# A two-number tile moved from the constants' pool to the temporaries' pool, so that the split weights start at multiples of 64 bytes

## The chip, the core and the metric

The kernel runs on one core of a Trainium2 chip. The metric is the device time of one execution in microseconds (us), the median of several runs. TensorE (PE) multiplies matrices, VectorE (DVE) and ScalarE (ACT) work element by element, SyncE (SP) issues most transfers from the main memory (HBM). Tiles lie in SBUF, 128 partitions wide; an address below is a byte address within each partition, the same on all 128.

## The reference

A decoder trunk of two layers on 256 tokens of 1024 numbers, all in float32. Every sublayer is wrapped in a norm, a modulation by a condition `c`, and a gated residual.

```python
def gated_post_add(x, y, g_post, gate, weight):
    return x + weight * gate[:, None, :] * rms_norm(y, g_post)

for layer in range(DEPTH):                       # DEPTH = 2
    ...
    y = swiglu_ffn(h, ffn_w_in[layer, 0], ffn_w_out[layer, 0])   # 1024 -> 2 x 2816 -> 1024
    x = gated_post_add(x, y, g[0, 1], mod[:, 0, 2], 0.5)
    ...
    if layer < n_a:
        y = short_conv_mixer(h, a_w_in[layer], a_conv[layer], a_w_out[layer])
    else:
        y = nsa_mixer(h, kv_cmp, kv_slc, kv_win, b_w_in[layer - n_a], b_w_out[layer - n_a])
    ...
    y = swiglu_ffn(h, ffn_w_in[layer, 1], ffn_w_out[layer, 1])
    ...
```

So there are four feed-forward sublayers, a short convolution, a sparse attention with its key and value side, and the modulations `silu(c) @ ada_w`.

## The kernel before

The tokens lie along the free dimension (256 columns) and the features on the 128 partitions. Each float32 product is made of three matmuls in the type fp32r: a weight block is split into a high part `whi` and the rest `wlo`, the activations into `hh`/`hl` (or `Hh`/`Hl` for the inner 2816 features), and `mm3` (L213) adds `hh` times `whi` (L215), `hl` times `whi` (L216) and `hh` times `wlo` (L217) in PSUM. In these the weights are the stationary operand (128 rows, 128 columns, loaded by a weight load of its own) and the activations are the moving operand (256 columns). Every matmul thus comes with a new weight load. Only where the values of the attention are projected (L652 to L654) the two are exchanged: `hh` and `hl` are loaded as weights and `whi` and `wlo` move.

The weights come in blocks of 2048 columns, loaded into `raw` (three buffers, SP's queue, L82). ScalarE copies a unit of 1024 columns into `whi` (L94), VectorE subtracts it from `raw` into `wlo` (L106); there are six buffers of each. VectorE also makes the modulations' products from blocks `graw` (L169). The norms sum squares by matmuls in which the data is the stationary operand and a single column of `ones` moves (`colsum`, L276); the attention's transposes (L878 to L880 and others) use an identity matrix that is part of the tile `sm`.

Four pools are stacked in SBUF in this order: `const` (x, z, hh, hl, then small tiles), `wp` (raw, whi, wlo), `tmp`, `gp` (graw), and behind these one that is exchanged (`hp` with Hh and Hl, `ap` for the attention). Each tile takes a multiple of 32 bytes. The tile `sxt` (two numbers for each partition, the sums of x squared; 8 bytes, so 32 with the rounding) is made in `const` (L986), written twice outside and inside of `sum_x_fin` (L1023, L287) and read by VectorE where the next norm's sums are worked out (`nc.vector.tensor_add(w, a1, self.sx)`, L381).

The order of the work is written out by hand; the pools set addresses and waits, not the order.

Of the kernel before, what the change touches and what calls it, by code (L numbers as in the profile page):

```python
# [9 lines left out]
F32 = mybir.dt.float32  # L10
# [12 lines left out]

# scale, shift and gate of each sublayer (and of the keys' and values' side) among the modulations
ADA = [(1, 0, 2), (4, 3, 5), (7, 6, 8), (10, 9, None), (19, 18, 11), (13, 12, 14), (16, 15, 17)]


class Trunk:
# [22 lines left out]

# [1 line left out]
    def w_init(self):  # L53
# [32 lines left out]
    def w_hi(self, upto):  # L86
        """the high parts, a unit ahead of the low ones"""
        while self.n_hi < min(upto, len(self.units)):
            i, u = self.units[self.n_hi]
            self.w_dma(i + 1)  # L90
            if i not in self.raw:
                return
            hi = self.wp.tile([128, 1024], F32R, name="whi", bufs=self.UNITS)
            self.nc.scalar.activation(hi, self.raw[i][:, u * 1024:u * 1024 + 1024], AF.Copy)  # L94
            self.his[self.n_hi] = hi
            self.n_hi += 1
# [18 lines left out]
    def w_whole(self):  # L115
        """the next block that is used as it is, and the function that frees it"""
        i = self.whole[0]
        self.w_dma(i + 1)

        def free():  # L120
            self.whole.pop(0)
            self.raw.pop(i)
            self.w_dma(i + 1 + self.RAW)
        return self.raw[i], free
# [7 lines left out]
    def w_ahead(self, more=0):  # L132
        """splits into what the units before the last taken one leave"""
        self.w_split(self.n_use + self.UNITS - 1 + more)

# [1 line left out]
    def g_init(self):  # L137
        """blocks of two columns of the modulations; scale and shift of a sublayer go together"""
        o = []
        for sub in range(7):  # L140
            sc, sh, gt = ADA[sub]
            o += [((sc, k), (sh, k)) for k in range(KC)]
            if gt is not None:
                o += [((gt, k), (gt, k + 1)) for k in range(0, KC, 2)]
        self.g_order = o
        self.g_raw = {}
        self.n_gd = self.n_g = 0
        self.credit = 0.0
        self.g_hold = False
        self.g_count = dict.fromkeys(range(20), 0)  # L150
        self.g_done = set()
# [28 lines left out]
    def g_fin(self, m, k0, k1):  # L180
        """with the bias; scales and gates times the norms' weights"""
        nc = self.nc
        v = self.mod[:, m, k0:k1]
        nc.vector.tensor_add(v, v, self.modb[:, m, k0:k1])
        if m >= 18:
            if m == 19:
                nc.vector.scalar_tensor_tensor(v, v, 1.0, self.kvg[:, k0:k1], op0=OP.add, op1=OP.mult)
        else:
            l, r = divmod(m, 9)
            s, p = divmod(r, 3)  # L190
            if p == 1:
                nc.vector.scalar_tensor_tensor(v, v, 1.0, self.ng[:, l, s, 0, k0:k1], op0=OP.add, op1=OP.mult)
            elif p == 2:
                nc.vector.scalar_tensor_tensor(v, v, 1.0 if s == 1 else 0.5, self.ng[:, l, s, 1, k0:k1],
                                               op0=OP.mult, op1=OP.mult)
        self.g_done.add(m)
# [14 lines left out]

# [1 line left out]
    def mm3(self, out, wh, wl, xh, xl, start, stop):  # L213
# [5 lines left out]
    def proj(self, hh, hl, n=1, nc_=2, each=None, out=None):  # L219
        """n weight blocks of [8 k, nc_ * 128 columns]; k is the outer loop. One bank for each."""  # L220
        out = out or [self.ps.tile([128, 2, S], F32, name="gu", bufs=4) for _ in range(n)]
# [24 lines left out]

# [1 line left out]
    def tiny(self, name):  # L248
        return self.tmp.tile([128, 2], F32, name=name)

    def inverse(self, s, name, late=False):
        """(s / D + eps) ** -0.5 of sums s [128, 2]: the mean of root / v and 1 / root, in which the root's error cancels"""
        nc = self.nc
# [12 lines left out]
    def spread(self, r, tag):  # L266
        """[128, 2] of the tokens -> [128, 256], the same on every partition"""
        o = self.ps.tile([128, S], F32, name=tag, bufs=4 if tag == "gu" else 2)
        for h in range(2):
            self.nc.tensor.transpose(o[:, h * 128:h * 128 + 128], r[:, h:h + 1].to_broadcast([128, 128]), self.ident)  # L270
        return o

    def colsum(self, o, v, start, stop):
        """o [128, 2] += the sums of v [128, 256] over the partitions, token 128 h + p at [p, h]"""
        for h in range(2):
# [3 lines left out]
    def sum_x(self):  # L279
        """sum of x ** 2 per token"""  # L280
        nc = self.nc
# [29 lines left out]
    def post_chunk(self, d, y):  # L311
        """z = y * gate * g and the sums of y ** 2, z ** 2 and x z"""
        nc = self.nc
# [12 lines left out]
    def post_mid(self):  # L326
        """the sums over all but the last chunk"""
        yy = self.ps.tile([128, 2], F32, name="st", bufs=2)
# [8 lines left out]
    def post_steps(self, nxt, keep=False):  # L337
        """x += r z; nxt: None or (scale, shift, hh, hl, blocks of the first wave) of the next sublayer.
        Without a first wave the steps are for the caller to spread over other work."""
        nc = self.nc  # L340
# [34 lines left out]
        ma, mb, hh, hl = nxt[:4]  # L375
        # the sum of (x + r z) ** 2 is x2 + 2 r xz + r ** 2 z2
        a1, w, a2, a3 = (self.tiny(n) for n in ("a1", "wx", "a2", "a3"))
# [49 lines left out]

# [1 line left out]
    def ffn(self, ia, fresh_x, nxt, kv=False):  # L429
        """ia: index of the sublayer's shift among the modulations"""  # L430
        nc = self.nc
# [157 lines left out]

# [1 line left out]
    def swap(self, name):  # L591
        """the large part of the memory to a new pool"""
        self.big.close()
        return self.big.enter_context(self.tc.tile_pool(name=name, bufs=1))
# [19 lines left out]
    def kv_proj(self):  # L614
# [4 lines left out]
        def each():  # L619
            """after each half of a block: a step of the queries' side"""  # L620
            half[0] ^= 1
            self.w_ahead(-1 - half[0])
            next(self.steps, None)
# [3 lines left out]
        for e in range(2):  # L627
            b = self.proj(hh, hl, each=each)[0]
            # group g on both halves of the partitions, the upper half one token ahead
            kc = self.BD[:, 4 * e:4 * e + 4].rearrange("p (a b) n -> p a (b n)", a=2)  # L630
# [30 lines left out]
    def blocks_of(self, e):  # L661
        """the compressed blocks' inputs [128 (2 tokens, 64), 16 token pairs, 4 groups, 15 blocks]"""
        at = 1024 * e
# [7 lines left out]
    def compress(self):  # L671
        """hidden units of the compressed blocks, (group, block) on partitions"""
        nc = self.nc
# [33 lines left out]
    def cmp_keys(self):  # L707
        """compressed keys [128 (2 groups, 64), 2 pairs, 32 (2 groups, 16 blocks)], block diagonal"""
        nc = self.nc
# [39 lines left out]
    def cmp_soft(self, a):  # L749
        """compressed branch: gated probabilities, transposed: [128 (4 chunks, 2 heads, 16 blocks), 2, 256 queries]"""  # L750
        nc = self.nc
# [31 lines left out]
    def q_half(self, i, u):  # L783
        """queries over -8, two heads (of groups 2 a and 2 a + 1) for each chunk; half of the products of two chunks"""
        nc = self.nc
# [190 lines left out]
    def run(self):  # L976
# [8 lines left out]
        self.sc = self.gp.tile([128, D], F32, name="sc")  # L985
        self.sx = c.tile([128, 2], F32, name="sxt")  # L986
        self.mod = c.tile([128, 20, 8], F32, name="mod")
# [97 lines left out]
def lay(inp):  # L1085
    """The inputs as the kernel wants them laid out; no arithmetic."""
    f = {n: np.asarray(v) for n, v in inp.items()}
# [17 lines left out]
    def cols128(w):  # L1105
        """[1024, 1024] -> blocks [128 p, 2 column chunks, 8 k, 128]"""
        v = w.reshape(KC, 128, 4, 2, 128)
        return ca(v.transpose(2, 1, 3, 0, 4)).reshape(4, 128, 2048)

    def cols256(w, pairs):  # L1110
        """[1024, n] -> blocks [128 p, 8 k, 256] of the columns that pairs names"""
        v = w.reshape(KC, 128, -1).transpose(1, 0, 2)
# [30 lines left out]
def consts(heads):  # L1143
    """Constants of the shapes alone: distances, penalties and masks."""
    big = 1e32
# [32 lines left out]
```

## Time and profile before

| | |
|---|---|
| runs | 1080.97, 1084.96, 1086.55 us; median 1084.96 us |
| profiled execution, from first to last instruction | 1084.8 us (the profile gives no other time of it) |
[...]
| TensorE busy | 96% of the span, 8438 matmuls |
| VectorE, ScalarE busy | 79%, 51% |
| HBM | 241 GB/s over the span |

"Busy" counts an instruction from its start to its end. Matmuls overlap each other: one of them takes 0.28 us from start to end, but the next one starts long before that. How fast TensorE gets on is seen only from how many matmuls start in a stretch of time.

### The profile page before, as it was taken

How to read it: one execution, taken by the hardware profiler on the slowest of the kernel's cores; microseconds unless marked ns; L12 is line 12 of the kernel's file. 1: busy time of each engine (PE TensorE's matmuls, PEld its weight loads, DVE VectorE, ACT ScalarE, POOL GpSimd, SP SyncE). 2: the span in 40 equal slices, each digit the busy share in tenths (PEclk: the TensorE clock that was granted, in tenths of full speed). 3: DMA queues.
4: the chain of work that ended last, by engine and by line, in shares of the span. 5: the costliest groups of instructions: out<-in, count | busy, mean ns of one | idle time of the engine just before them, and what ended most of it. 6: DMA issues, size and time to landing. Idle time of an engine off the chain costs nothing.

```text
span 1084.8 us, 20601 instructions
## 1 busy us (share of the span) xinstructions
PE 1042.1 (96%) x8438; PEld 1014.2 (93%) x8438; DVE 857.3 (79%) x1618; ACT 550.9 (51%) x1006; POOL 5.0 (0%) x12
## 2 busy tenths in 40 slices
PE   4999999999999999999999999999999999999996
PEld 4899999999989999998999999998887789999996
DVE  6879889799888988897898878968678698555553
ACT  3544454444556444554644444633578746444541
POOL 0000000000000000000000000010000000000000
PEclk9999999989989999999999999999999989999998
DMA  9899989727644988896298885766532134555531
GB/s 379 348 350 376 347 322 366 295 79 272 232 157 176 369 342 316 298 349 246 96 385 335 332 312 214 280 225 237 229 113 83 55 135 165 197 190 193 195 118 39
DMA packets 38063, 264.30 MB, mean 244 GB/s; under 512 B 4304, under 2 KB 5584, under 8 KB 6736
## 3 DMA queue, kind: packets, MB, share of 16 engines
q1 hardware_dynamic: 37584, 261.94, 64.2%
q8 instruction: 66, 1.08, 0.4%
q0 software_dynamic: 384, 1.05, 0.4%
q14 instruction: 29, 0.24, 0.1%
HBM read 260.87 MB, written 1.05 MB: 241 GB/s over the span
## 4 chain that ended last, share of the span: by engine, by line
PE 89%; DVE 7%; ACT 2%; issue 1%; DMA 1%; DVEq 0%; SPq 0%; ACTq 0%
PE gu L215 18%; PE gu L217 17%; PE gu L216 17%; PE y L215 9%; PE y L216 9%; PE y L217 9%; DVE graw L169 2%; PE st L276 2%; PE y L684 1%; PE gu L235 1%; PE gu L825 1%; DVE wlo L106 1%; DVE e L298 1%; PE y L891 1%; DMA x<-in_x_dram 1%
## 5 line engine op out<-in xcount | busy, mean ns | idle before, releaser
L215 PE MATMUL gu<-hh,whi 128*128 128x256 f32 x1592 | 447.9, 281 | 0.0
L216 PE MATMUL gu<-hl,whi 128*128 128x256 f32 x1592 | 446.2, 280 | 0.0
L217 PE MATMUL gu<-hh,wlo 128*128 128x256 f32 x1592 | 446.1, 280 | 0.0
L106 DVE TENSOR_TENSOR wlo<-raw,whi 128x1024 fp32r<-128x1024 f32 x319 | 379.1, 1221 | 60.4 <-ACT whi L94 60.4
L94 ACT ACTIVATE whi<-raw 128x1024 fp32r<-128x1024 f32 x319 | 323.6, 1054 | 47.7 <-PE y L216 31.0
L215 PEld LDWEIGHTS gu<-hh,whi 128*128 128x128 f32 x1592 | 301.4, 189 | 0.0
L216 PEld LDWEIGHTS gu<-hl,whi 128*128 128x128 f32 x1592 | 301.3, 189 | 0.0
L217 PEld LDWEIGHTS gu<-hh,wlo 128*128 128x128 f32 x1592 | 300.9, 189 | 0.0
L215 PE MATMUL y<-Hh,whi 128*128 128x256 f32 x768 | 217.1, 283 | 3.0 <-ACT st L318 3.0
L216 PE MATMUL y<-Hl,whi 128*128 128x256 f32 x768 | 216.5, 282 | 0.0
L217 PE MATMUL y<-Hh,wlo 128*128 128x256 f32 x768 | 216.4, 282 | 0.0
L169 DVE SCALAR_TENSOR_TENSOR graw<-graw,sc 128x1024 f32<-128x1024 f32 x160 | 194.1, 1218 | 0.0
L215 PEld LDWEIGHTS y<-Hh,whi 128*128 128x128 f32 x768 | 145.4, 189 | 3.4 <-ACT st L318 3.4
L216 PEld LDWEIGHTS y<-Hl,whi 128*128 128x128 f32 x768 | 145.5, 189 | 0.0
L217 PEld LDWEIGHTS y<-Hh,wlo 128*128 128x128 f32 x768 | 145.5, 189 | 0.0
L445 ACT ACTIVATE e<-gu 128x256 f32<-128x256 f32 x88 | 33.4, 380 | 197.0 <-PE gu L217 197.0
L446 DVE TENSOR_TENSOR e<-gu,e 128x256 f32<-128x256 f32 x88 | 37.2, 423 | 56.9 <-ACT e L445 56.7
L316 ACT ACTIVATE st<-y 128x256 f32<-128x256 f32 x42 | 16.1, 383 | 76.9 <-PE y L217 76.9
L302 ACT ACTIVATE hh<-e,mod 128x256 fp32r<-128x256 f32 x36 | 18.3, 510 | 61.8 <-DVE e L298 61.8
L319 DVE TENSOR_TENSOR st<-z,x 128x256 f32<-128x256 f32 x42 | 17.8, 424 | 36.0 <-ACT z L317 35.8
L450 ACT ACTIVATE Hh<-e 128x256 fp32r<-128x256 f32 x88 | 36.1, 410 | 17.6 <-DVE e L446 17.5
L451 DVE TENSOR_TENSOR Hl<-e,Hh 128x256 fp32r<-128x256 f32 x88 | 37.0, 420 | 7.8 <-ACT Hh L450 7.8
(197 smaller groups left out, 992.4 us busy)
## 6 DMA issues: line engine op xcount, KB each, us to landing
raw<-in_wi_dram SPq DMA_DIRECT2D x85, 1024.0 KB, 6.1
graw<-in_ada_dram SPq DMA_DIRECT2D x80, 1024.0 KB, 7.3
raw<-in_wo_dram SPq DMA_DIRECT2D x44, 1024.0 KB, 5.4
raw<-in_cu_dram SPq DMA_DIRECT2D x8, 1024.0 KB, 6.0
raw<-in_kvw_dram SPq DMA_DIRECT2D x6, 1024.0 KB, 7.3
raw<-in_bb_dram SPq DMA_DIRECT2D x4, 1024.0 KB, 5.2
raw<-in_ao_dram SPq DMA_DIRECT2D x4, 1024.0 KB, 4.8
raw<-in_w_dram SPq DMA_DIRECT2D x4, 1024.0 KB, 4.8
```

Source lines behind the costliest of these rows:

```text
L94: self.nc.scalar.activation(hi, self.raw[i][:, u * 1024:u * 1024 + 1024], AF.Copy)
L106: self.nc.vector.tensor_sub(lo, self.raw[i][:, u * 1024:u * 1024 + 1024], hi.bitcast(F32))
L169: nc.vector.scalar_tensor_tensor(w, w, 1.0, self.sc, op0=OP.mult, op1=OP.mult, accum_out=self.mod[:, m, k:k + 1])
L215: mm(out, wh, xh, start=start, stop=False, skip_group_check=True)
L216: mm(out, wh, xl, start=False, stop=False, skip_group_check=True)
L217: mm(out, wl, xh, start=False, stop=stop, skip_group_check=True)
L276: self.nc.tensor.matmul(o[:, h:h + 1], v[:, h * 128:h * 128 + 128], self.ones[:, 0:1], start=start and h == 0, stop=stop and h == 1, skip_ ...
L302: self.nc.scalar.activation(hh[:, k, :], t, AF.Identity, bias=self.mod[:, mb, k:k + 1])
L445: nc.scalar.activation(sg, b[:, 0, :], AF.Silu)
L446: nc.vector.tensor_mul(hf[f], b[:, 1, :], sg)
L450: nc.scalar.activation(H[:, f, :], t, AF.Copy)
L451: nc.vector.tensor_sub(L[:, f, :], t, H[:, f, :].bitcast(F32))
```

## The change

The tile `sxt` is made in the pool `tmp`, with one buffer, where it was made in `const`. The rest of the diff removes comments and leaves their lines empty, so that line numbers stay.

```diff
@@ -983,7 +983,7 @@
         self.hh = c.tile([128, KC, S], F32R, name="hh")
         self.hl = c.tile([128, KC, S], F32R, name="hl")
         self.sc = self.gp.tile([128, D], F32, name="sc")
-        self.sx = c.tile([128, 2], F32, name="sxt")
+        self.sx = self.tmp.tile([128, 2], F32, name="sxt", bufs=1)
         self.mod = c.tile([128, 20, 8], F32, name="mod")
         self.ones = c.tile([128, 128], F32, name="ones")
         self.eps = c.tile([128, 1], F32, name="eps")
```

Both programs hold the same instructions in the same order on every engine, with the same waits; only addresses differ. What lies ahead of `sxt` stays, what lies between its old and its new place moves down by 32 bytes, and what lies behind its new place stays, since the 32 bytes come in again there:

| tiles | first address before | bytes past a multiple of 64 | first address after | bytes past a multiple of 64 |
|---|---|---|---|---|
| x, z, hh, hl | 16512 | 0 | 16512 | 0 |
| mod | 49312 | 32 | 49280 | 0 |
| ones | 49952 | 32 | 49920 | 0 |
| the identity in sm | 51776 | 0 | 51744 | 32 |
| raw (3 of 8192 bytes) | 52320 | 32 | 52288 | 0 |
| whi (6 of 4096 bytes) | 76896 | 32 | 76864 | 0 |
| wlo (6 of 4096 bytes) | 101472 | 32 | 101440 | 0 |
| sxt | 49280 | 0 | 126016 | 0 |
| e, st, acc and the rest of tmp's large tiles but one | 128160 | 32 | 128160 | 32 |
| graw; Hh, Hl; the attention's mh, ml, q, KC, KT, w2 | 157504 and on | 0 | the same | 0 |

## Rows read from the trace of the kernel before

**Rows 1.** The page, part 1: busy time, share, instructions.

```profile
PE 1042.1 (96%) x8438; PEld 1014.2 (93%) x8438; DVE 857.3 (79%) x1618; ACT 550.9 (51%) x1006; POOL 5.0 (0%) x12
```

**Rows 2.** The page, part 4: the chain that ended last, by engine.

```profile
PE 89%; DVE 7%; ACT 2%; issue 1%; DMA 1%; DVEq 0%; SPq 0%; ACTq 0%
```

**Rows 3.** Groups of TensorE's matmuls by line and form: the products.

```profile
L215 PE MATMUL gu<-hh,whi 128*128 128x256 f32 x1592 | 447.9, 281 | 0.0
...
L215 PE MATMUL y<-Hh,whi 128*128 128x256 f32 x768 | 217.1, 283 | 3.0 <-ACT st L318 3.0
...
L215 PE MATMUL y<-mh,whi 128*128 128x256 f32 x64 | 19.3, 301 | 0.0
...
L215 PE MATMUL y<-hh,whi 128*128 128x256 f32 x64 | 18.0, 282 | 0.0
...
L652 PE MATMUL gu<-whi,hh 128*128 128x256 f32 x32 | 9.0, 281 | 0.0
...
L215 PE MATMUL gu<-mh,whi 128*128 128x256 f32 x8 | 2.4, 295 | 0.0
```

**Rows 4.** Windows with matmuls alone: stretch, length, busy (count), clock, DMA.

```profile
50.00:147.00 97.00, 97.00 (x826) 1.00 0.95 360
152.00:209.00 57.00, 57.00 (x484) 1.00 0.87 334
...
327.00:443.00 116.00, 116.00 (x988) 1.00 0.81 308
448.00:505.00 57.00, 57.00 (x484) 1.00 0.85 318
530.00:632.00 102.00, 102.00 (x877) 1.00 0.86 321
...
736.20:747.20 11.00, 11.00 (x95) 1.00 0.63 235
...
901.00:1008.00 107.00, 107.00 (x920) 1.00 0.54 197
1013.00:1070.00 57.00, 57.00 (x484) 1.00 0.31 112
```

**Rows 5.** Groups of weight loads by form; names: moving operand, then the loaded one.

```profile
L215 PEld LDWEIGHTS gu<-hh,whi 128*128 128x128 f32 x1592 | 301.4, 189 | 0.0
...
L276 PEld LDWEIGHTS st<-ones,acc 128*128 128x128 f32 x64 | 8.3, 191 | 0.5 <-DVE acc L323 0.5
...
L652 PEld LDWEIGHTS gu<-whi,hh 128*128 128x128 f32 x32 | 6.0, 188 | 0.0
...
L746 PEld LDWEIGHTS y<-KC,q 128*128 128x128 f32 x32 | 3.8, 192 | 0.2
...
L734 PEld LDWEIGHTS st<-w,e 128*128 128x128 f32 x8 | 1.0, 191 | 0.0
```

**Rows 6.** Timeline of weight loads in a row: start, length of all, count.

```profile
783.26 1.86 PEld L746 LDWEIGHTS y<-KC,q 128*128 128x128 f32 x16
```

```profile
214.25 0.97 PEld L276 LDWEIGHTS st<-ones,st 128*128 128x128 f32 x8
```

**Rows 7.** The page, part 5: the split, and the modulations' products.

```profile
L106 DVE TENSOR_TENSOR wlo<-raw,whi 128x1024 fp32r<-128x1024 f32 x319 | 379.1, 1221 | 60.4 <-ACT whi L94 60.4
...
L169 DVE SCALAR_TENSOR_TENSOR graw<-graw,sc 128x1024 f32<-128x1024 f32 x160 | 194.1, 1218 | 0.0
```

**Rows 8.** Waits: engine and line, whom for, us in total, times, longest.

```profile
DVE wlo L106 <- ACT whi L94: 60.4, 72, 5.4
...
ACT whi L94 <- DMA raw<-in_wi_dram: 9.1, 2, 7.1
```

## The prediction

> **What bounds the kernel now.** First the page's busy times and the chain that ended last [rows 1, 2]: TensorE is busy for 96% of the span and makes up 89% of the chain; VectorE has 7% of it, ScalarE 2%, DMA 1%. So the time is that in which TensorE works through its matmuls, plus the start and the norms. Then the matmuls by line [rows 3]: the products of split weights are 1592 + 768 + 64 + 64 + 8 triples of L215 to L217 and 32 triples of L652 to L654, that is 2528 × 3 = 7584 of the 8438 matmuls. Their mean of 280 ns is no price, since they overlap. The price is the step from one start to the next, and it is read from windows [rows 4]. A window counts every matmul that lies in it in part, so the step is (length + 0.28 us) / count. In the up-projection of the four feed-forward sublayers it is 97.28 / 826 = 117.8 ns, 116.28 / 988 = 117.7, 102.28 / 877 = 116.6 and 107.28 / 920 = 116.6; in three of their down-projections 57.28 / 484 = 118.3. [...] Over the eight windows together it is (604 + 8 × 0.28) / 5158 = 117.5 ns. 7584 steps of 117.5 ns are 891 us of the 1084.8.
>
> This sets the scale of the whole question: one nanosecond of this step is worth 7.6 us, and 0.5% of the time (5.4 us) is 0.72 ns of it. About 0.5% is also what a measurement of this kernel can tell from no change; the three runs shown lie 0.5% apart themselves.
>
> **The change part by part.** No instruction is added, removed or reordered, and no queue is passed, so every term is a duration that might depend on an address.
>
> The tile `sxt` itself: it has its only buffer for the whole program in either pool, so its new place brings no wait for another tile. VectorE writes and reads two numbers of it once or twice for each sublayer, as before. Cost: nothing. The other small tiles that move (mod, ones, eps) are read as scalars or single columns; the identity goes the other way, from a multiple of 64 to 32 past one. It is the moving operand of the 130 transposes that the program holds. If that cost as much as the largest difference between the steps of rows 4, 118.3 − 116.6 = 1.7 ns each, it would be 0.2 us; it is left at 0.
>
> VectorE and ScalarE on raw, whi and wlo: the subtraction at L106 has all three operands 32 past a multiple of 64 and takes 1221 ns; the product at L169 of the same 1024 columns has all of its operands on a multiple and takes 1218 ns [rows 7]. So the most that alignment could give is 3 ns × 319 = 1 us of VectorE's time, and that lies beside TensorE's: VectorE waits for ScalarE's whi 72 times, and TensorE's windows show no idle time at all while they do [rows 4, 8]. Value taken: 0. Without that cover it would be the same 1 us.
>
> The transfers into raw: ScalarE waited for one of them twice, 9.1 us in total [rows 8], and the chain has 1% of DMA [rows 2]. The transfers' shares in rows 4 (0.31 to 0.95) do not go with the steps: 117.8 ns at a share of 0.95, 118.3 at 0.31. Value taken: 0.
>
> The weight loads and the matmuls, the term that matters. What alignment does to a weight load can be read in this trace, since it holds weight loads of both kinds of tile [rows 5]. From tiles 32 past a multiple of 64: 189 ns for whi, 191 for acc, 191 for e (L734). From tiles on a multiple: 188 for hh (L652), 192 for q (L746). No difference beyond 1 or 2 ns, in either sense. Durations of overlapping instructions are weak evidence, so the step is better. Where the moving operand is short, loads follow each other as fast as they can [rows 6]: sixteen from q, on a multiple, take 1.86 us, so (1.86 − 0.19) / 15 = 111.3 ns apart; eight from st, 32 past, take 0.97 us, so (0.97 − 0.19) / 7 = 111.4 ns apart. A load is not slowed by the 32 bytes. The moving operand: at L652 to L654 the roles are exchanged, the loaded operand lies on a multiple and whi moves, 32 past. The step there is 11.28 / 95 = 118.7 ns, within the counting error of 1.2 ns the same as with the roles as usual [rows 4]. So the operand that is misplaced is sometimes the loaded one, sometimes the moving one, and the step does not tell which.
>
> One gap stays. Every product has exactly one operand of the split weights, so no row shows a full stream with both operands on a multiple of 64. Bounds: below, the step of loads alone, 111.4 ns, which is what is left if all of the excess came from the offset, 7584 × (117.5 − 111.4) = 46 us gained; nothing in the rows gives less than that. Above, an excess that both operands on the same offset would cause; the nearest rows are the two sizes of step that this very program shows with its addresses unchanged. The up-projection of the first sublayer and that of the third have the same lines, the same hh and hl, the same buffers of weights, and 117.8 and 116.6 ns. So the step has levels that an address does not choose, about 1.2 to 1.7 ns apart; one level above the highest would be 118.3 + 1.7 = 120.0 ns, 7584 × 2.5 = 19 us lost. Between these I take 117.5, no change, because the loads at both offsets, the nearest rows to the disputed operation, are equal to a tenth of a nanosecond.
>
> [...]
>
> **Sum.** 0 for sxt and the small tiles, 0 for VectorE and ScalarE, 0 for the transfers, 0 for 7584 steps: 1084.8 us for the profiled execution. It stands 0.16 us below the runs' median of 1084.96, so the forecast is 1084.9 us.
>
> **The rivals.**
>
> *Both operands on a multiple bring the step down to what the loads alone need.* For it: the products' step is 6 ns above that of loads alone, and in the whole program no product has both operands aligned. Against it: loads of either offset go at the same pace, and the exchanged roles change nothing. 7584 × 6.1 = 46 us less: 1039 us.
>
> *The levels fall.* New addresses might let every stretch settle at the fast level that only two of the four up-projections have now. For it: the levels exist, and they differ between stretches that do the same. Against it: with addresses unchanged they already differ, so addresses are not what picks them. 7584 × (117.5 − 116.6) = 7 us less: 1078 us.
>
> *The levels rise.* All stretches settle at the level that the down-projections have: 7584 × (118.3 − 117.5) = 6 us more, 1091 us. For and against as before.
>
> *Slower: loaded and moving operand meet.* Now they start at the same offset within 64 bytes, where before they were 32 apart, and are read at the same time. If this puts each step one level higher, to 120.0 ns, it is 1104 us. For it: in this program products never had that before, and the excess of the step over the loads' 111.4 ns shows that something between the two readings costs time. Against it: acc, st and ones in L276 had the same offset, and q and KC in L746 too, with loads at 111.4 and 111.3 ns, though there little moves. It decides from 0.72 ns of step on.
>
> **How the numbers follow.** No effect on the step, with levels wandering by a few us from run to run: 0.59, of it nearly all within 0.5%. Down to the loads' pace: 0.12. Levels fall: 0.13. Levels rise: 0.07. Operands meet: 0.09. Faster by over 0.5% gets the first and second rival, 0.25. Slower by over 0.5% gets the last two less a little for the third, which is close to the limit: 0.14. Within 0.5%: 0.61. The range leaves out the ends, 1039 and 1104 us with 0.12 and 0.09, and holds the rest with room for the levels: 1072 to 1096 us. No change by itself, the likeliest, would lie within 1080 to 1090.
>
> **What would show it.** Right: windows in the same stretches with 116.6 to 118.4 ns for each step, weight loads of whi at 189 ns, L106 at 1220 ns, the norms as before. If the offset matters, it shows in the windows of the up- and down-projections alike, as counts that rise by 5% (111.4 ns) or fall by 2% (120.0 ns), while L652 to L654 show the same change, since there both operands are aligned as well now. If only the levels moved, some windows show 116.6 and others 118.3 in another distribution than in rows 4, and the loads alone keep their 111 ns. The prediction is wrong if a step outside of 116.6 to 118.4 ns appears, or if VectorE or a transfer shows up in the chain where TensorE was.

## The result, and the profile after

The changed kernel takes 1090.93 us (median of 10 runs, 1087.41 to 1093.89), the kernel before 1084.32 us (median of 10, 1077.61 to 1087.38). The ratio is 1.0065, with a 95% interval of 1.0042 to 1.0088. It became slower by 0.65%, clear of the noise.

The profiled execution spans 1092.1 us where that of before spans 1084.8. Its page, busy times and the chain by engine, to be held against [rows 1, 2]:

```profile
span 1092.1 us, 20601 instructions
PE 1049.7 (96%) x8438; PEld 1020.8 (93%) x8438; DVE 857.8 (79%) x1618; ACT 551.5 (50%) x1006; POOL 5.0 (0%) x12
...
PE 90%; DVE 6%; ACT 2%; issue 1%; DMA 0%; DVEq 0%; ACTq 0%
```

TensorE is busy 7.6 us longer with the same 8438 matmuls, which is all of the 7.3 us by which the span grew. VectorE and ScalarE differ by less than 1 us. So the place to look is the step from one matmul to the next. Windows with matmuls alone, the same stretches as [rows 4] but for the one of L652 to L654, which lies later now (739 to 749):

```profile
50.00:147.00 97.00, 97.00 (x826) 1.00 0.94 363
152.00:209.00 57.00, 57.00 (x477) 1.00 0.87 324
327.00:443.00 116.00, 116.00 (x988) 1.00 0.80 302
448.00:505.00 57.00, 57.00 (x478) 1.00 0.83 311
530.00:632.00 102.00, 102.00 (x869) 1.00 0.82 311
739.00:749.00 10.00, 10.00 (x91) 1.00 0.59 224
901.00:1008.00 107.00, 107.00 (x912) 1.00 0.52 187
1013.00:1070.00 57.00, 57.00 (x478) 1.00 0.37 135
```

The step is again (length + 0.28 us) / count. The down-projections went from 118.3 ns to 57.28 / 477 = 120.1 and 57.28 / 478 = 119.8. The first two up-projections stay at 117.8 and 117.7; the last two, which had 116.6, are now at 117.7 and 117.6 too. L652 to L654 went the other way, from 118.7 to 10.28 / 91 = 113.0 ns. In such a window one matmul more or less is a quarter of a nanosecond in the down-projections, an eighth in the up-projections, and 1.2 ns in the short window of L652 to L654. So three groups of the same kind of matmul moved by different amounts, one of them downwards, at a granted clock of 1.00 in all of these windows.

Weight loads by group, of the changed kernel:

```profile
L215 PEld LDWEIGHTS gu<-hh,whi 128*128 128x128 f32 x1592 | 301.4, 189 | 0.0
...
L215 PEld LDWEIGHTS y<-Hh,whi 128*128 128x128 f32 x768 | 147.4, 192 | 2.9 <-ACT st L318 2.9
...
L276 PEld LDWEIGHTS st<-ones,acc 128*128 128x128 f32 x64 | 8.3, 191 | 0.3 <-DVE acc L323 0.3
```

The same tile `whi` is loaded in 189 ns while hh moves and in 192 ns while Hh moves; before it was 189 in both (the page before lists 145.4 us for the 768 loads). Where nothing much moves, the loads follow each other as before. Timeline of weight loads in the norm behind the first feed-forward, the changed kernel:

```profile
215.27 0.97 PEld L276 LDWEIGHTS st<-ones,st 128*128 128x128 f32 x8
```

It is the 0.97 us of [rows 6]: 111.4 ns from load to load. No change shows where a single column moves; the one that shows is in the loads of whi beside the 256 columns of Hh.

The work of the other engines is not needed for it. In the last down-projection there is a stretch in which VectorE, ScalarE and the transfers do nothing at all. That stretch with the first and the last of 37 matmuls in it, in the changed kernel and then in the kernel before (busy time of TensorE, its weight loads, VectorE, ScalarE and GpSimd, then clock and transfers):

```profile
1068.10:1072.50 4.40, 4.40 (x39) 4.40 (x39) 0.00 (x0) 0.00 (x0) 0.00 (x0) 1.00 0.00 0
...
1068.16 0.28 PE L216 MATMUL y<-Hl,whi 128*128 128x256 f32 x1
...
1072.48 0.28 PE L216 MATMUL y<-Hl,whi 128*128 128x256 f32 x1
```

```profile
1061.00:1065.30 4.30, 4.30 (x39) 4.30 (x38) 0.00 (x0) 0.00 (x0) 0.00 (x0) 1.00 0.00 0
...
1061.02 0.28 PE L216 MATMUL y<-Hl,whi 128*128 128x256 f32 x1
...
1065.28 0.28 PE L216 MATMUL y<-Hl,whi 128*128 128x256 f32 x1
```

36 steps in 4.32 us are 120.0 ns, and 36 in 4.26 us are 118.3: the same as with the other engines at work.

### The profile page after: what moved, and what is told of

The parts are those of the page before. It is cut to its first block, busy times and chain, and to the rows that moved or that the text cites. A ratio compares the mean times of both kernels' runs of the same rounds, so it can differ in the third digit from the quotient of the medians.

```text
span 1092.1 us, 20601 instructions
## 1 busy us (share of the span) xinstructions
PE 1049.7 (96%) x8438; PEld 1020.8 (93%) x8438; DVE 857.8 (79%) x1618; ACT 551.5 (50%) x1006; POOL 5.0 (0%) x12
## 4 chain that ended last, share of the span: by engine, by line
PE 90%; DVE 6%; ACT 2%; issue 1%; DMA 0%; DVEq 0%; ACTq 0%
PE gu L215 17%; PE gu L216 17%; PE gu L217 17%; PE y L215 9%; PE y L216 9%; PE y L217 9%; DVE graw L169 2%; PE st L276 2%; PE gu L825 1%; PE y L684 1%; PE gu L235 1%; PE y L891 1%; DVE wlo L106 1%; DVE e L298 1%; PE gu L828 1%
## 5 line engine op out<-in xcount | busy, mean ns | idle before, releaser
L106 DVE TENSOR_TENSOR wlo<-raw,whi 128x1024 fp32r<-128x1024 f32 x319 | 379.1, 1221 | 59.2 <-ACT whi L94 58.7
L302 ACT ACTIVATE hh<-e,mod 128x256 fp32r<-128x256 f32 x36 | 18.3, 510 | 61.8 <-DVE e L298 61.8
```

The source lines that it names most:

```text
L106: self.nc.vector.tensor_sub(lo, self.raw[i][:, u * 1024:u * 1024 + 1024], hi.bitcast(F32))
L302: self.nc.scalar.activation(hh[:, k, :], t, AF.Identity, bias=self.mod[:, mb, k:k + 1])
```

## The experiments

Theory A: the step is set by the difference between the start of the loaded operand and that of the moving one. Theory B: it is set by whether the split weights themselves start on a multiple of 64 bytes. A third possibility is that the moved tile itself costs something. In all of these kernels the products are the same; padding tiles that nothing reads or writes shift what lies behind them.

**e1, e2, e3: shift one side, or both.**

```diff
# e1: the changed kernel; Hh, Hl and the attention's tiles 32 bytes higher
+        self.gp.tile([128, 8], F32, name="padg")
         nc.vector.memset(self.ones, 1.0)
# e2: the kernel before, with the same line
# e3: the changed kernel; everything 32 bytes higher
+        c.tile([128, 8], F32, name="pad0")
         self.x = c.tile([128, KC, S], F32, name="x")
```

Expected of e1: 

> The changed kernel with 32 bytes of padding behind graw, so that Hh, Hl and the attention's tiles start 32 bytes higher; whi, wlo, hh and hl stay where the change put them (whi on a multiple of 64). Theory A, the step depends on the offset between the operand that moves and the one that is loaded: the down-projections leave 120.0 ns for each matmul and come to about 118.3 as before, the up-projections stay at 117.8; some 4 us less than the changed kernel. Theory B, the step depends on whether the split weights themselves start at a multiple of 64: all windows as in the changed kernel, 117.8 and 120.0 ns.

Expected of e2: 

> The kernel before (sxt in the constants' pool, whi 32 past a multiple of 64) with the same 32 bytes of padding behind graw: whi and Hh are now both 32 past a multiple of 64, their difference that of the changed kernel. Theory A: the down-projections go to 120.0 ns for each matmul, the up-projections stay as before (116.6 to 117.8). Theory B: 118.3 ns in the down-projections as before.

Expected of e3: 

> The changed kernel with 32 bytes of padding ahead of x: every tile starts 32 bytes higher, so the split weights lie 32 past a multiple of 64 as before, and every difference between two tiles is that of the changed kernel. Theory A: as the changed kernel, 117.8 ns in the up- and 120.0 in the down-projections, about 1090 us. Theory B: as the kernel before, 116.6 to 117.8 and 118.3 ns, about 1084 us.

Measured, one run each: e1 1086.78 us, e2 1088.17 us, e3 1088.14 us, beside 1083.95 us for the kernel before on the same chip. Windows of the first up- and the first down-projection, e1, then e2, then e3:

```profile
50.00:147.00 97.00, 97.00 (x826) 1.00 0.94 363
152.00:207.00 55.00, 55.00 (x474) 1.00 0.87 332
```

```profile
50.00:147.00 97.00, 97.00 (x833) 1.00 0.94 364
152.00:207.00 55.00, 55.00 (x460) 1.00 0.88 329
```

```profile
50.00:147.00 97.00, 97.00 (x826) 1.00 0.93 363
152.00:207.00 55.00, 55.00 (x460) 1.00 0.86 322
```

e3 decides it. Its weights lie 32 past a multiple of 64, just as in the kernel before, and its steps are those of the changed kernel, 117.8 and 55.28 / 460 = 120.2 ns. e2 leaves the weights of the kernel before where they are and reaches 120.2 ns in the down-projection by moving Hh alone. e1 has the weights where the change put them and gets down to 55.28 / 474 = 116.6 ns by moving Hh alone. Theory B falls. Theory A expected about 118.3 for e1, by taking a shift of 32 to either side for the same; it is not.

**e4, e5, e6: other differences.**

```diff
# the kernel before; e5: n = 24, m = 56; e6: n = 32, m = 32 (e4: the changed kernel, n = 16, m = 32)
+        c.tile([128, n], F32, name="padc")
         self.mod = c.tile([128, 20, 8], F32, name="mod")
...
+        self.gp.tile([128, m], F32, name="padg")
         nc.vector.memset(self.ones, 1.0)
```

Expected of e4: 

> The changed kernel with 64 bytes of padding behind hl and 128 behind graw: every tile named here on a multiple of 64, but the difference of whi and hh is now a multiple of 512 (448 past one in the changed kernel) and that of whi and Hh 128 past one (256 in the changed kernel). Theory A: both kinds of windows change; if a meeting at the same place is what costs, the up-projections rise above 117.8 ns. Theory B: as the changed kernel, 117.8 and 120.0 ns.

Expected of e5: 

> The kernel before with 96 bytes of padding behind hl and 224 behind graw: whi lies 64 bytes past a multiple of 256 behind hh, Hh and mh alike; all of these on multiples of 64. Theory A, the step is set by the difference of the two operands' addresses modulo 256: 113.5 ns for each product, as L652 to L654 showed at a difference of 64 in the changed kernel, so 7488 x (117.5 - 113.5) = 30 us less than before, 1054 us. Rival, the 113.5 ns belong to the exchanged roles of L652 alone: 117 to 120 ns here, within 10 us of the kernel before.

Expected of e6: 

> The kernel before with 128 bytes of padding behind hl and 128 behind graw: a difference of 96 modulo 256 between whi and hh, of 160 between whi and Hh. Theory A: two values of the step not yet seen, each the same in all of its windows; a smooth course from 113.5 at 64 to 118.7 at 128 would give about 116 for 96, and one from 118.7 at 128 to 117.8 at 192 about 118 for 160. Theory B, the split weights' own start: as the kernel before, since they lie 32 past a multiple of 64.

e4 took 1100.93 us, e6 1095.39 us (one run each). e5 took 1076.7 us (median of 9), ratio 0.9935 to the kernel before, interval 0.9903 to 0.9968: faster than both kernels, but by 7 us where 30 were expected. Counted through, the convolution is the second sublayer, and the second, third and last feed-forward are the third, fourth and sixth. Windows of e4 (first up- and down-projection), of e6 (the same, and the up-projection of the third sublayer), then of e5 (the first sublayer's up- and down-projection, then the up-projections of the third and of the fourth sublayer, each ahead of and behind the sums of L276 in it, at 339 and 534 us):

```profile
50.00:147.00 97.00, 97.00 (x811) 1.00 0.93 356
152.00:207.00 55.00, 55.00 (x466) 1.00 0.88 328
```

```profile
50.00:147.00 97.00, 97.00 (x820) 1.00 0.93 360
152.00:207.00 55.00, 55.00 (x460) 1.00 0.88 321
...
341.00:430.00 89.00, 89.00 (x762) 1.00 0.87 325
```

```profile
50.00:147.00 97.00, 97.00 (x859) 1.00 0.95 372
147.00:202.00 55.00, 55.00 (x488) 1.00 0.92 350
...
317.00:338.50 21.50, 21.50 (x192) 1.00 0.33 110
341.00:430.00 89.00, 89.00 (x758) 1.00 0.92 350
...
510.00:533.00 23.00, 23.00 (x205) 1.00 0.35 120
536.00:630.00 94.00, 94.00 (x800) 1.00 0.92 349
```

e4 puts the up-projections, at a difference of 0, to 97.28 / 811 = 120.0 ns. All windows of e4 and e6 moved, though every tile of e4 lies on a multiple of 64. In e5 the step of the first up-projection is 97.28 / 859 = 113.2 ns, the value that L652 to L654 had in the changed kernel, so it does not belong to their exchanged roles. But in the third sublayer it is 21.78 / 192 = 113.4 ns up to the sums and 89.28 / 758 = 117.8 ns behind them, and in the fourth 23.28 / 205 = 113.6 and 94.28 / 800 = 117.9. Timeline of TensorE in e5 at the place of the change:

```profile
339.09 0.28 PE L217 MATMUL gu<-hh,wlo 128*128 128x256 f32 x1
339.20 0.95 PE L276 MATMUL st<-ones,sx 128*128 128x1 f32 x8
340.01 0.36 PE L215 MATMUL gu<-hh,whi 128*128 128x256 f32 x1
```

Nothing but the eight short matmuls of L276 stands between the two. In the first sublayer, which has no such sums there, the step stays at 113 ns (55.28 / 488 = 113.3 in the down-projection). So some differences allow two levels, and an interruption of the stream can change which of them holds. It need not: in the kernel before, the sums in the convolution changed the step from 24.28 / 206 = 117.9 ns (230 to 254 us) to 31.78 / 272 = 116.8 (257 to 288.5 us), while the window of 530 to 632 us in [rows 4] has such sums in it, too, and stays at 116.6.

In e4 the difference of the down-projections is 128, and there the level changes where the products wait twice for ScalarE (1.0 and 1.9 us), in the fourth sublayer. First and last matmul of a stretch ahead of these waits (196 matmuls), and of one behind them (145):

```profile
651.82 0.28 PE L217 MATMUL y<-Hh,wlo 128*128 128x256 f32 x1
...
674.96 0.28 PE L217 MATMUL y<-Hh,wlo 128*128 128x256 f32 x1
...
695.72 0.28 PE L216 MATMUL y<-Hl,whi 128*128 128x256 f32 x1
...
713.00 0.28 PE L216 MATMUL y<-Hl,whi 128*128 128x256 f32 x1
```

That is 23.14 / 195 = 118.7 ns, then 17.28 / 144 = 120.0.

**e7, e10: the two parts of the change, one without the other.** e7 moves sxt as the change does and pads its old place, so that the weights stay relative to hh and Hh modulo 256. e10 leaves sxt and gives the differences of the changed kernel.

```diff
# e7: the changed kernel, n = 8, m = 56; e10: the kernel before, n = 56, m = 8
+        c.tile([128, n], F32, name="padc")
...
+        self.gp.tile([128, m], F32, name="padg")
```

Expected of e7: 

> sxt in the temporaries' pool as in the change, with 32 bytes of padding in its old place and 224 behind graw: whi, wlo, hh and hl lie where they lay before the change, Hh 256 bytes higher than in the kernel before relative to whi. Theory A with 256 as the period: steps as in the kernel before, 116.6 to 117.8 and 118.3 ns, and its time within 0.5%. Theory A with 512 as the period: the down-projections show some other step. If the place of sxt itself costs something: the norms longer and the time 5 us or more above before with the steps of before.

Expected of e10: 

> The kernel before, sxt in its old place, with 224 bytes of padding behind hl and 32 behind graw: the differences of the changed kernel modulo 256 (192 for hh, 0 for Hh) without its edit. Theory A: 117.8 and 120.0 ns, and the ratio of the changed kernel, 1.004 to 1.009. Theory B: the weights lie on multiples of 64, so the same by that; if the moved tile was the cause: as the kernel before.

e7: 1084.43 us, ratio 0.9999 (0.9972 to 1.0027). e10: 1090.63 us, ratio 1.0060 (1.0037 to 1.0083). Windows of the first up- and down-projection, e7, then e10:

```profile
50.00:147.00 97.00, 97.00 (x834) 1.00 0.96 366
152.00:207.00 55.00, 55.00 (x467) 1.00 0.86 329
```

```profile
50.00:147.00 97.00, 97.00 (x826) 1.00 0.95 363
152.00:207.00 55.00, 55.00 (x461) 1.00 0.86 320
```

Moving the tile costs nothing (e7), and the differences without the moved tile cost what the change costs (e10: 117.8 and 55.28 / 461 = 119.9 ns). Modulo 512, the difference of whi and Hh is 32 in e7 and 288 in the kernel before; their steps are 55.28 / 467 = 118.4 and 118.3 ns. With 0 and 256 both at 120 ns (the up-projections of e4, the down-projections of e10), two pairs agree with 256 as the period, and none speaks against it.

**e8, e9: the sums of L276 later.** In both the call that sums the new x is moved out of the up-projections and the convolution's projection to the last eighth of the down- or output projection; e8 is e5 with it, e9 the kernel before with it.

```diff
-            if fresh_x and f == 4:
-                self.sum_x_fin()
...
+                if fresh_x and d == 7 and f == 5:
+                    self.sum_x_fin()
...
-            if i == 5:
-                self.sum_x_fin()
...
+            if mg == 5 and d == 7:
+                self.sum_x_fin()
```

Expected of e8: 

> e5 with the matmuls of L276 that sum the new x (eight, in the third block of the up-projections and of the convolution) moved to the last eighth of the down-projection or of the output projection. In e5 the step was 113.3 ns up to these matmuls and 117.8 behind them. Theory C, such an interruption sends the stream from one of two levels that a difference of 64 allows to the other: 113.3 to 113.5 ns in nearly all windows, 3 x 820 + 280 up- and 3 x 525 + 190 down-projection steps shorter by 4.4 ns, about 20 us less than e5, 1055 us. Rival, the level changes by itself after some time: as e5, 1070 to 1080 us, with the change at another place in each window.

Expected of e9: 

> The kernel before with the same sums moved, no padding. Theory C and the table of differences: 118.3 ns in the down-projections, 116.6 or 117.8 in the up-projections, so within 0.5% of the kernel before. If moving the sums saves time by itself: faster with the steps of before.

e8: 1069.49 us, ratio 0.9834 (0.9801 to 0.9867), five of its six runs between 1059.57 and 1072.18 us. e9: 1079.6 us, ratio 0.9949 (0.9932 to 0.9965). Windows of e8 in the first sublayer, in the up- and down-projection of the third, and in the up-projection of the last; then the first and last of 86 matmuls at L652 to L654 in e8:

```profile
50.00:147.00 97.00, 97.00 (x826) 1.00 0.94 357
152.00:207.00 55.00, 55.00 (x469) 1.00 0.90 339
...
341.00:430.00 89.00, 89.00 (x788) 1.00 0.94 361
450.00:488.00 38.00, 38.00 (x338) 1.00 0.90 342
...
901.00:985.00 84.00, 84.00 (x715) 1.00 0.55 196
```

```profile
718.76 0.28 PE L654 MATMUL gu<-wlo,hh 128*128 128x256 f32 x1
...
728.40 0.28 PE L652 MATMUL gu<-whi,hh 128*128 128x256 f32 x1
```

The third sublayer keeps 89.28 / 788 = 113.3 ns behind the old place of the sums and 38.28 / 338 = 113.3 in its down-projection. But the first sublayer, which had 113 ns in e5, is at 117.8 here from its start to its end, and the last is at 84.28 / 715 = 117.9. So the sums did switch the level in e5, as theory C says, and the stretches of e8 that are not interrupted there kept theirs: 113.3 ns in both windows of the third sublayer, 117.8 and 55.28 / 469 = 117.9 in those of the first. What sets the level at the start of a stretch these runs do not show. The two sublayers that started at the upper one here hold some 3000 products, which at 4.5 ns are 13 us: most of what e8 lacks to the 1055 us that were expected. e8 gained 15 us on the kernel before and is the fastest of these kernels.

At L652 to L654 e8 has a difference of 192 and a step of 9.64 / 85 = 113.4 ns, where the changed kernel has 117.8 in all of its up-projections at this difference. So 192 has two levels as well, the same two as 64.

e9 gained a little more than the 0.5% that was expected to be its limit. In its trace every up-projection has the lower of the two levels that this difference shows: the first one 97.28 / 833 = 116.8 ns, that of the third sublayer 89.28 / 766 = 116.6. In the trace before, two of the four had the upper one; 1.1 ns on their some 2000 products are about 2 us of the 5 that e9 gained. Whether moving the sums gives something by itself, in e9 and so in e8 too, is not shown.

**The table that comes out.** Difference = start of the loaded tile minus start of the moving one, modulo 256 bytes; the step is that of the windows.

| difference | step, ns | where |
|---|---|---|
| 0 | 119.7 to 120.2 | changed kernel, e2, e3, e10 down; e4 up |
| 32 | 118.3 to 118.4 | before, e7 down; L652 before, 118.7 on 95 matmuls |
| 64 | 113.2 to 113.6, or 117.7 to 117.9 | e5, e8; L652 in the changed kernel, 113.0 on 91 |
| 96 | 117.2, or 118.6 | e6 up |
| 128 | 118.7, or 120.0 | e4 down |
| 160 | 119.6 to 120.2 | e6 down |
| 192 | 117.6 to 117.9, or 113.4 | changed kernel, e1, e3, e10 up; L652 in e8 |
| 224 | 116.6 to 116.8, or 117.7 to 117.9 | before, e2, e7, e9 up; e1 down |

These are the steps that were seen. A difference with one entry may have a second level that no stretch here was in, as 192 seemed to have one level until e8.

Before the change the pairs were 224 (hh) and 32 (Hh); the change made them 192 and 0. L652 to L654, with the roles exchanged, went from 32 to 64.

## Why the prediction was wrong

**The terms that held.** The tile itself (written at L294 and L1023 and read at L380, not at L287 and L381 as stated ahead) costs nothing that e7 shows (0.9999, interval 0.9972 to 1.0027). The scalars and the identity lie in e7 where they lay before the change, so that run says nothing of them; in the traces before and after, the instructions that read mod as a scalar take the same (L302 510 ns, L298 476 ns), and the transposes of L879 and L880 have a median of 273 ns in both. Those of L878 went from 300 and 312 ns to 328 and 326, in a part of the attention where the clock differed too, so a cost of the identity's place there is not shown apart from the clock. VectorE's split takes 1221 ns as before, and VectorE, ScalarE and the transfers have no more of the chain (6%, 2% and 0%) than in [rows 2].

**The step that failed** is the last term, "7584 steps at 0". It measured 6 us, as worked out below, and the prediction's own sign of being wrong, a step outside of 116.6 to 118.4 ns, appeared on both sides: 120.0 in the down-projections, 113.0 at L652 to L654. It was reasoned in three moves. The first, that loads by themselves follow each other at 111 ns at either offset, is right and was measured again (0.97 us for eight). But it says nothing of loads beside a stream of 256 columns, and the text took "the nearest rows" as the measure all the same. The second was that L652 to L654 show the same step with exchanged roles, within a counting error of 1.2 ns. Exchanged roles turn the sign of the difference: 224 becomes 32, the very value of the down-projections, whose 118.3 ns they share. Those rows fit theory A and were read as evidence against it. The third was that the two levels among the up-projections, with the same addresses (117.8 in the first feed-forward, 116.6 in the third), show that addresses do not choose the level. They do not choose between the two that a difference allows, but they do choose which levels were seen: 116.6 and 117.8 ns at 224, 113.3 and 117.8 at 64.

**The scale was right.** By the seven stretches that both kernels share, the mean step went from (593 + 1.96) / 5063 = 117.51 to 594.96 / 5028 = 118.33 ns; 0.82 ns on the 7488 products other than L652 to L654 is 6.1 us of the 7.3. The other 1.2 us need no step. The attention is longer in the trace after by 2.7 us: its last matmuls of L746 lie 2.2 us behind those of the trace before, its last ones of L891 4.9 us, and between them a part ran at a granted clock of 0.50 (820 to 826 us). Windows in it, before, then after:

```profile
810.00:830.00 20.00, 20.00 (x144) 1.00 0.41 159
```

```profile
810.00:830.00 20.00, 20.00 (x124) 0.83 0.40 159
```

e3, with the differences of the changed kernel, has 147 matmuls at 1.00 in this window, and e7, with those of before, has less than the full clock around it (0.86 from 805 to 830 us), so this goes with the execution and not with the change. The fourth down-projection gave some 2 us back: from 641 to 706 us it was the trace before that had the lower clock (0.97, 509 matmuls) and the one after the full (1.00, 520).

That 1090.9 us lies within the range that was given, 1072 to 1096, is luck: its upper part was made for levels that wander, not for a step of 120.0 ns.

**The rivals.** "Loaded and moving operand meet" came nearest: it has the step go by how the two operands lie to each other, and names the windows in which that would be read. But it counted offsets modulo 64 and so charged all 7584 steps, 19 us. At a difference of 0 modulo 256 are only Hh, Hl, mh and ml: (768 + 64 + 8) × 3 = 2520 steps of about 1.6 ns are 4.0 us. The rest is the loss of the lower level in the up-projections, 1.1 ns on two of them, some 2 us. Its 120.0 ns, the highest step plus the distance of two levels, was met by luck, and meeting is not all of it: 160 costs the same (e6). "The levels rise" gave 1091 us, the measured time, by luck: it had all windows at 118.3 ns, and none is.

**What stays open.** Why 256 bytes, and why 64 and 192 have the lowest step and 0 and 160 the highest, no run here shows, nor whether the readings of the two operands disturb each other. Nor is it known what picks the level at the start of a stretch. e1 to e4 and e6 are one run each, so their times are weak; their steps are read from hundreds of matmuls each.

## What to carry to other kernels

Where each matmul loads new weights, as here, its step can depend on how the loaded and the moving tile lie to each other (113.2 to 120.2 ns in these runs), not on a round address of either (e3, e4): look at the difference of the two starts modulo 256, and read the step as a count of matmuls in a window that is long enough to tell half a nanosecond, with no norm in it. A small tile ahead of the weights shifts that difference by 32 bytes, which cost 0.65% here, far from where the tile is used. If a row is to show that something does not matter, see first whether in that row it differs.

## What was not expected of the hardware

- The step between products of the same form took values from 113.2 to 120.2 ns at a granted clock of 1.00, by the difference of two addresses and, at the same difference, by the level that a stretch was in.
- At a difference of 64 two steps, 113.3 and 117.8 ns, each held for a whole stretch of some hundred matmuls and more; at 224 there were 116.6 and 117.8. Eight short matmuls in between sufficed to go from one to the other (e5).
- The least that any long product stream showed here is 113.2 ns (e5, 859 matmuls); none came down to the 111.4 ns at which loads follow each other beside a single moving column.
- 32 bytes in the difference, from 32 to 0, moved the step of the down-projections from 118.3 to 120.0 ns.
